# The last of four mLSTM heads: its instructions on VectorE, ScalarE and GpSimd put into a written order

## The chip, the core and the metric

The kernel runs on one NeuronCore of one Trainium2 chip, in one launch. The time is that of the device, in microseconds, from three runs; the profile is one further execution. The engines run their own in-order queues and meet only through semaphores: TensorE (PE, with its weight loads shown apart as PEld), VectorE (DVE), ScalarE (ACT), GpSimd (POOL), and SP, which here issues nearly all transfers.

## The reference

One layer of a hybrid backbone, batch 1, 1024 latent tokens (`x`) and 256 context tokens (`ctx`), width 1024. Only the latent stream is returned. Cut to what matters here:

```python
# adaLN-modulated RMSNorm, then one projection into all parts
hm, _, _ = mlstm_bidirectional(qm, km, vm, gates_x, st_f, st_b, True)     # 4 heads of width 128
y_m = mlstm_merge(hm, om, mlstm_norm[l])
y_a = window_attention(apply_rope(qa, cos, sin) * attn_scale, apply_rope(ka, cos, sin), va,
                       ka_c, va_c, attn_sink[l])                          # 8 query heads of width 64
x = x + g_a * (jnp.concatenate([y_m, y_a], axis=-1) @ w_out[l])
x = x + g_f * conv_glu(modulate(rmsnorm(x, norm_ffn[l]), sh_f, sc_f), ...)

def mlstm_merge(h, o, gain):
    hn = h * lax.rsqrt(jnp.mean(h * h, axis=-1, keepdims=True) + EPS)
    hn = hn.transpose(0, 2, 1, 3).reshape(b, l, MLSTM_W) * gain
    return (hn * jax.nn.sigmoid(o)).astype(o.dtype)
```

The mLSTM runs over chunks, forward and backward. Each chunk of a head has a state (128x128 matrix and a vector) from the chunks before it, and an inner part in which every pair of positions has a decay, an exponential under a causal mask. The output of a position is the sum of both directions, each divided by its own normaliser. `mlstm_merge` then divides by the root of the mean square over the 128 elements of the head, and multiplies by a gain and by the sigmoid of an output gate.

## The kernel before

**Stages.** First norm, modulation and shared projections; then the four mLSTM heads, one after the other; while head h runs its recurrence, TensorE does the dense projections of head h+1 (`dense`), and during the last head, which has no successor, the query projections of the attention (`qgen`). Then window attention with the output projection, then the convolutional GLU. A tile has 128 partitions; a chunk here is 128 tokens, so there are 8 latent chunks (`NL`) and 2 context chunks (`NC`).

**One head** is the generator `mlstm`. It `yield`s 30 times. Between two yields the loop at the bottom of the listing lets `dense` or `qgen` add some TensorE work: it keeps a debt, raised by `RATE` (1.5) or, in the last head, `RATE3` (0.37) per yield, and takes pieces of 0.64 from the other generator until the debt is paid. A query projection is four such pieces. In the order of the yields, counted n = 0 to 29:

- n = 0, 1: two chunks of k are transposed ahead (`tr`, L653), and ScalarE copies them out with two scales (L657, L659).
- n = 2 to 10: nine backward state steps, i = 0 to 8. Each transposes two chunks ahead, multiplies (L680), and VectorE adds to the state (L688, L690). Here stand also the loads of the decays' exponents (`ee_load`), the additions of the causal mask (`mask`, L663), the exponentials (`decay`, L667, ScalarE), the pieces in which the head before is finished (`next(fins[0])`), and the output gate: tanh on ScalarE over all 8 chunks (L703) and a product on VectorE (L704).
- n = 11, 12: two forward state steps over the context. n = 13: the first q-k product.
- n = 14 to 29: eight turns of two yields, one per latent chunk, numbered 0 to 7 here. `first` makes the q-k product of the next chunk and the next forward state (L722, L710, L715), and multiplies decays in (L725). `second` makes the output (L733 to L736 on TensorE), ScalarE scales the state's part (L739), VectorE adds (L740) and makes the normalisers (L742 to L744). Its `rest` comes one turn later: ScalarE and VectorE form `hid` (L747, L748), and, a yield later, ScalarE squares and sums it (L751) into `hss`.

```python
        for c in range(NC, NCH):
            if c + 1 < NCH:
                first(c + 1)
            if tail:
                next(tail)
            yield
            ...
            if tail:
                next(tail)
            tail = second(c)
            yield
```

`finish` ends a head: root of the mean square on ScalarE (L784, another activation table than the exponential's and the tanh's), reciprocal (L785), and eight scalings of 128x128 (L787) on VectorE. For heads 0 to 2 it is spread over the state steps of the next head; for the last head it follows at once.

**PSUM.** The transposes, state steps, q-k products and outputs of a head share one pool of four buffers (`pl`). After the last head that pool is closed and its four banks go to the attention's pools (`pT`, `pO`, `pU`), which the rest of `qgen` already uses for the transposes of q and k (L883, L857). In the same place the head's scratch memory is closed, and `wm` opens in it: the attention's keys (`kT2`), values (`vv`) and the output weights (`wor`). The first write there is ScalarE's L1032.

**Order.** The framework has a planner that orders each engine's instructions by estimated times. Inside `tc.manual_schedule(engines=...)` the engines named issue in the order in which the code writes them; how that region mixes with instructions written outside it stays with the planner. The loop over heads names TensorE always, and for heads 0 to 2 also VectorE, ScalarE, GpSimd and SP. So in the last head only TensorE has a written order.

**Query projections.** Weights for queries come in two sets. The second, `w_q[1]`, is loaded in the last head by `load_split`: two halves of 512 KB (L152), each cut into a high part (copy on ScalarE, L156) and a low part (subtraction on VectorE, L157). Each projected chunk is rotated by three VectorE instructions (L319, L319, L320), which free one of two PSUM buffers; then `qtrans` splits (L877 on ScalarE, L878 on VectorE), transposes, copies out (L885) and stores q (L886).

Of the kernel before, what the change touches and what calls it, by code (L numbers as in the profile page):

```python
# [9 lines left out]
F32 = mybir.dt.float32  # L10
# [8 lines left out]
P = 128  # L19
# [59 lines left out]
def build(tc, I, out, dbg=None):  # L79
# [553 lines left out]
    fins = []  # L633

    def mlstm(h, kT, qT, va):
# [32 lines left out]

        ahead = [tr(order[1][0])]
# [4 lines left out]
        for i, c in enumerate(order[1][:-1]):  # L674
# [22 lines left out]
            if i > 1:  # L697
                mask(i - 2)
            if i in (4, 6, 8):
                decay(i // 2 - 2)  # L700
            if i == TN:

                S.activation(yv, yv, AF.Tanh, scale=0.5)  # L703
                V.scalar_tensor_tensor(out=yv, in0=yv, scalar=1.0, in1=rwc("gain", h * DH, DH).unsqueeze(1)  # L704
                                       .broadcast_to([P, NL, DH]), op0=ALU.add, op1=ALU.mult)
# [22 lines left out]
        def second(c):  # L728
# [17 lines left out]
            def rest():  # L746
                S.activation(hid[:, b], nm[:, 0, 0:DH], AF.Copy, scale=dn[:, 0:1])  # L747
                V.scalar_tensor_tensor(out=hid[:, b], in0=nm[:, 1, 0:DH], scalar=dn[:, 1:2], in1=hid[:, b],  # L748
                                       op0=ALU.mult, op1=ALU.add)
                yield  # L750
                S.activation(nm[:, 0, 0:DH], hid[:, b], AF.Square, accum_out=hss[:, b:b + 1])  # L751
                yield
            return rest()

        for c in range(NC):
            pn = pl.tile([P, 512], F32, name="pn", tag="l")
            step(c, pn[:, 0:E1])
            if c == 0:
                cfs.clear()
            if c == 0:  # L760
                mask(NL - 1)
            decay(3 + c)
            yield
        first(NC)
        tail = None
# [27 lines left out]
        if h < H - 1:  # L793
            fins.append(finish())
        else:
            for _ in finish():
                pass

# [175 lines left out]
    for h in range(H):  # L977
# [3 lines left out]
        else:  # L981
            wq = [wkq]
            late = lambda: wq.append(load_split(I["w_q"][1], 256, lambda: pq.tile([P, 4, 256], F32, name="wr", tag="rga")))
# [14 lines left out]
        with tc.manual_schedule(engines=order_):  # L998
            dn = dense(h + 1, wkq, wvo, *nh) if nh else qgen()
            rate = RATE if nh else RATE3  # L1000
            for n, _ in enumerate(mlstm(h, *cur)):
                if nh is None and n == LW3:
                    late()
                    rga = pq.tile([P, D], F32, name="rga", tag="rga")
                    nc.sync.dma_start(rga[:], row(0))
# [17 lines left out]
            if nh is None:  # L1023
                mstk.close()
# [1158 lines left out]
```

## Time and profile before

| | us |
|---|---|
| three runs: lowest, median, highest | 1265.94, 1266.54, 1266.77 |
| profiled execution, its own time | 1265.89 |
| its span, first to last instruction | 1264.1 |
| mean granted TensorE clock | 0.998 |
| first mLSTM instructions of the last head, about | 322 |
| last scaling of the last head (L787) ends | 362.3 |

How to read the lines that follow: a timeline row has the start in us, the length in us, the engine, the line, the operation, output <- inputs, and the number of instructions merged; in brackets the idle time before it and what ended it. The length of one instruction runs from its start to its end, and the next may start before that end. A wait row names the engine, tile and line that waited, the one it waited for, the sum in us, how often, and the longest. PEld shows TensorE's weight loads, one for each product.

### The profile page before, as it was taken

Reading aid. Unit: us, or ns where it says so; the run is one execution under the profiler, and the core shown is the slowest. Engines: PE = TensorE matmul, PEld = TensorE weight load, DVE = VectorE, ACT = ScalarE, POOL = GpSimd, SP = SyncE. Lnnn points to the kernel's source line nnn. Section 1 sums busy time; section 2 is a strip of 40 time slices with the busy share of each in tenths; the row PEclk is TensorE's granted clock in tenths of the full one; section 3 lists DMA queues with packets and bytes.
Section 4 is the critical chain, followed back from the end, with each engine's and each line's share of the span. In section 5 each row is a group of like instructions: output and inputs, shape, how many; then the busy total and the mean of one; then the engine's idle time right before and its main releaser. Section 6 shows DMA issues by size and latency. Waiting matters only on the chain.

```text
span 1264.1 us, 19253 instructions
## 1 busy us (share of the span) xinstructions
PE 1234.4 (98%) x7047; PEld 1060.2 (84%) x7047; DVE 972.8 (77%) x1691; ACT 637.9 (50%) x1309; POOL 187.1 (15%) x162
## 2 busy tenths in 40 slices
PE   6999999999999999999999999999999999999997
PEld 4799999999898888888887888888888888788886
DVE  5873777777787888788987877777777777877887
ACT  6632556464865777776843333333333334434435
POOL 1200000000001443221002232133231232001000
PEclk9999999999999999999999999999999999999999
DMA  9541535362354333104313322223322237975553
GB/s 361 184 142 34 145 115 153 115 181 75 85 175 160 134 120 115 51 34 167 117 51 130 115 99 102 95 102 117 103 105 100 93 135 269 335 250 187 195 192 134
DMA packets 90560, 176.17 MB, mean 139 GB/s; under 512 B 12954, under 2 KB 29538, under 8 KB 90466
## 3 DMA queue, kind: packets, MB, share of 16 engines
q1 hardware_dynamic: 90178, 174.15, 41.2%
q8 instruction: 56, 0.92, 0.3%
q10 hardware_dynamic: 288, 0.79, 0.2%
q14 instruction: 38, 0.31, 0.1%
HBM read 136.58 MB, written 38.33 MB: 138 GB/s over the span
## 4 chain that ended last, share of the span: by engine, by line
PE 84%; DVE 6%; ACT 5%; DMA 3%; issue 2%; POOL 1%; SPq 0%; ACTq 0%; DVEq 0%; POOLq 0%
PE pd L2020 14%; PE pa L1480 8%; PE pc L1480 8%; PE pp L588 7%; PE pe L1480 4%; PE pd L1480 4%; PE pb L1480 4%; PE u L1182 3%; PE pv L307 2%; PE pv L309 2%; PE pv L308 2%; PE po L307 2%; PE po L309 2%; PE po L308 2%; PE pt L1159 2%
## 5 line engine op out<-in xcount | busy, mean ns | idle before, releaser
L1597 ACT CAST wh<-Rb 128x1024 fp32r<-128x1024 f32 (+1 forms) x63 | 56.8, 903 | 144.1 <-PE pd L1480 77.1
L2020 PE MATMUL pd<-dh,al 128*128 128x512 f32 x296 | 115.4, 390 | 0.9 <-DVE al L1361 0.9
L2020 PE MATMUL pd<-dl,ah 128*128 128x512 f32 x296 | 115.3, 389 | 0.0
L2020 PE MATMUL pd<-dh,ah 128*128 128x512 f32 x296 | 115.1, 389 | 0.0
L1480 PE MATMUL pc<-hB,wh 128*128 128x512 f32 x344 | 105.6, 389 | 0.0
L1480 PE MATMUL pa<-hB,wh 128*128 128x512 f32 x336 | 103.8, 390 | 0.2 <-ACT sn L1679 0.2
L1198 DVE TENSOR_TENSOR wl<-Rb,wh 128x1024 fp32r<-128x1024 f32 (+1 forms) x63 | 65.8, 1045 | 39.2 <-ACT wh L1597 38.6
L1715 POOL TENSOR_TENSOR tt<-vt,tt 128x512 f32<-128x512 f32 x22 | 29.5, 1341 | 367.5 <-ACT tt L1709 367.5
L588 PE MATMUL pp<-hl,wh 128*128 128x512 f32 x256 | 79.3, 405 | 0.0
L307 PE MATMUL pv<-wh,hl 128*128 128x256 f32 x256 | 75.9, 296 | 0.0
L1480 PEld LDWEIGHTS pc<-hB,wh 128*128 128x128 f32 x344 | 64.6, 188 | 13.5
L1480 PEld LDWEIGHTS pa<-hB,wh 128*128 128x128 f32 x336 | 62.9, 188 | 14.1 <-ACT sn L1679 1.1
L309 PE MATMUL pv<-wh,hl 128*128 128x256 f32 x256 | 72.4, 283 | 0.0
L308 PE MATMUL pv<-wl,hl 128*128 128x256 f32 x256 | 72.3, 282 | 0.0
L2020 PEld LDWEIGHTS pd<-dh,al 128*128 128x128 f32 x296 | 55.6, 188 | 13.1 <-DVE al L1361 1.6
L1480 PE MATMUL pc<-hB,wl 128*128 128x512 f32 x172 | 66.4, 389 | 0.0
L2020 PEld LDWEIGHTS pd<-dl,ah 128*128 128x128 f32 x296 | 55.5, 188 | 11.8 <-DVE dl L1361 0.3
L1480 PE MATMUL pa<-hB,wl 128*128 128x512 f32 x168 | 65.4, 389 | 0.0
L2020 PEld LDWEIGHTS pd<-dh,ah 128*128 128x128 f32 x296 | 55.6, 188 | 11.6
L1166 ACT CAST ph<-pt 128x512 fp32r<-128x512 f32 (+1 forms) x88 | 46.2, 525 | 25.3 <-PE pt L1159 25.0
L1136 DVE TENSOR_REDUCE nm<-sps 128x1 f32<-128x641 f32 (+1 forms) x64 | 50.3, 786 | 4.9 <-PE sps L1132 3.4
L1480 PE MATMUL pd<-hB,wh 128*128 128x512 f32 x176 | 54.0, 390 | 0.0
(1082 smaller groups left out, 3694.4 us busy)
## 6 DMA issues: line engine op xcount, KB each, us to landing
w<-in_w_ada_dram SPq DMA_DIRECT2D x64, 256.0 KB, 2.8
br<-in_w_down_dram SPq DMA_DIRECT2D x25, 512.0 KB, 5.9
ar<-act_s SPq DMA_DIRECT2D x44, 256.0 KB, 4.0
Ra<-in_w_up_dram SPq DMA_DIRECT2D x21, 512.0 KB, 3.6
Rb<-in_w_up_dram SPq DMA_DIRECT2D x21, 512.0 KB, 3.6
act_a<-tt SPq DMA_DIRECT2D x33, 256.0 KB, 2.0
act_s<-tt SPq DMA_DIRECT2D x33, 256.0 KB, 2.0
wr<-in_w_h_dram SPq DMA_DIRECT2D x16, 512.0 KB, 4.1
```

What stands on the lines that cost most here:

```text
L307: T.matmul(ps, st_hi, mv_hi, start=first, stop=False)
L308: T.matmul(ps, st_hi, mv_lo, start=False, stop=False)
L309: T.matmul(ps, st_lo, mv_hi, start=False, stop=last)
L588: T.matmul(pp[:, 512 * n:512 * n + 512], wkq[sw][:, kt, cs], hl[n][part][:, kt, :], start=kt == 0 and sw + part == 0, stop=kt == KT - 1 an ...
L1136: V.tensor_reduce(out=self.nm[:, j:j + 1], in_=self.sv[j], axis=AX.X, op=ALU.max, negate=True)
L1166: S.copy(self.ph[i][:, :w], self.pt[i][:, :w])
L1182: T.matmul(self.u[:], vv[:, c, self.g], part[i][:, kk * 2 * P:(kk + 1) * 2 * P], start=kb + m == 0, stop=kb == last and m == 1)
L1198: sub = lambda e, o, x, y: e.tensor_tensor(out=o, in0=x, in1=y, op=ALU.subtract)
L1480: T.matmul(ps[:, cols], wt[sw][:, j, kt * P:kt * P + P], hB[part][:, blk, kt, cols], start=first and n == 0, stop=last and n == len(seq) - ...
L1597: S.copy(wt[0][:], src)
L1715: G.tensor_tensor(out=self.tt[:, h2_], in0=self.vt[:], in1=self.tt[:, h2_], op=ALU.mult)
L2020: T.matmul(ps[:], ac[sa][:, js], w[sw], start=first and n == 0, stop=last and n == 2, skip_group_check=not fresh)
```

## The change

- The last head gets a written order on VectorE, ScalarE and GpSimd too (`inner`), ended when its generator is exhausted. SP stays with the planner there.
- In the last head the masks and exponentials come two state steps later (`late_ = 2`), and the output gate (`gate`, the old L703 and L704) moves from the eighth state step to the square of chunk 2, that is, to n = 21.
- Head 2 isn't finished piece by piece in the last head. `gated` multiplies its hidden values by its gate in one 128x1024 VectorE instruction, written at i = 1, and keeps its sums of squares. The last head does the same at its end, and then both heads are finished together: two roots, two reciprocals, two products of 128x1024.
- `w_q[1]` is no longer loaded and cut in one place (n = 12). Its first half is issued at n = 6 and cut at n = 13, where the second is issued; that is cut at n = 20, and the row of the residual's gate (`rga`) is loaded there.

```diff
--- before.py
+++ after.py
@@ -630,7 +630,7 @@
         if h == 0:
             dump("kT", kT[:]); dump("qT", qT[:]); dump("va", va[:].rearrange("p c e -> p (c e)"))
 
-    fins = []
+    fins, held = [], []
 
     def mlstm(h, kT, qT, va):
         cbk = tp.tile([P, NL, DH + 1], F32, name="cbk", tag="cbk", bufs=1)
@@ -666,6 +666,12 @@
             for d in range(2):
                 S.activation(ee[:, b, d], ee[:, b, d], AF.Exp, bias=g1(a_, d, NC + b), scale=-1.0)
 
+        def gate():
+            S.activation(yv, yv, AF.Tanh, scale=0.5)
+            V.scalar_tensor_tensor(out=yv, in0=yv, scalar=1.0, in1=rwc("gain", h * DH, DH).unsqueeze(1)
+                                   .broadcast_to([P, NL, DH]), op0=ALU.add, op1=ALU.mult)
+
+        late_ = 2 if h == H - 1 else 0
         ahead = [tr(order[1][0])]
         yield
         ahead.append(tr(order[1][1]))
@@ -694,15 +700,12 @@
                 ee_load(2 * i + 2)
             if fins and i:
                 next(fins[0])
-            if i > 1:
-                mask(i - 2)
-            if i in (4, 6, 8):
-                decay(i // 2 - 2)
-            if i == TN:
-
-                S.activation(yv, yv, AF.Tanh, scale=0.5)
-                V.scalar_tensor_tensor(out=yv, in0=yv, scalar=1.0, in1=rwc("gain", h * DH, DH).unsqueeze(1)
-                                       .broadcast_to([P, NL, DH]), op0=ALU.add, op1=ALU.mult)
+            if i > 1 + late_:
+                mask(i - 2 - late_)
+            if i in (4 + late_, 6 + late_, 8):
+                decay((i - late_) // 2 - 2)
+            if i == TN and not late_:
+                gate()
             yield
         cf, cfs = [None], []
 
@@ -749,6 +752,8 @@
                                        op0=ALU.mult, op1=ALU.add)
                 yield
                 S.activation(nm[:, 0, 0:DH], hid[:, b], AF.Square, accum_out=hss[:, b:b + 1])
+                if late_ and b == 2:
+                    gate()
                 yield
             return rest()
 
@@ -757,11 +762,18 @@
             step(c, pn[:, 0:E1])
             if c == 0:
                 cfs.clear()
-            if c == 0:
-                mask(NL - 1)
-            decay(3 + c)
+            if late_:
+                mask(5 + c)
+                decay(2 + c)
+            else:
+                if c == 0:
+                    mask(NL - 1)
+                decay(3 + c)
             yield
         first(NC)
+        if late_:
+            mask(NL - 1)
+            decay(4)
         tail = None
         yield
         for c in range(NC, NCH):
@@ -790,15 +802,25 @@
                     yield
             fins.clear()
             yield
-        if h < H - 1:
+
+        def gated():
+            V.tensor_tensor(out=yv, in0=hid[:], in1=yv, op=ALU.mult)
+            held.append((hss, yv))
+            fins.clear()
+            yield
+        if h < H - 2:
             fins.append(finish())
+        elif h < H - 1:
+            fins.append(gated())
         else:
-            for _ in finish():
+            for _ in gated():
                 pass
-
-
-
-
+            for s_, _ in held:
+                S.activation(s_[:], s_[:], AF.Sqrt, bias=eps_t[:], scale=1.0 / DH)
+            for s_, _ in held:
+                V.reciprocal(s_[:], s_[:])
+            for s_, y_ in held:
+                V.tensor_tensor(out=y_, in0=y_, in1=s_[:].unsqueeze(2).broadcast_to([P, NL, DH]), op=ALU.mult)
 
     def ada_second():
         R4 = 4 * KT
@@ -980,7 +1002,8 @@
             order_ |= {mybir.EngineType.DVE, mybir.EngineType.Activation, mybir.EngineType.Pool, mybir.EngineType.SP}
         else:
             wq = [wkq]
-            late = lambda: wq.append(load_split(I["w_q"][1], 256, lambda: pq.tile([P, 4, 256], F32, name="wr", tag="rga")))
+            wq1 = lambda: load_split(I["w_q"][1], 256, lambda: pq.tile([P, 4, 256], F32, name="wr", tag="rga"), split=False,
+                                     alloc=False, now=(0,))
             for _ in ada:
                 pass
             V.scalar_tensor_tensor(out=ada2[:, 16:24], in0=ada2[:, 16:24], scalar=1.0, in1=spc("nffn", 0, KT), op0=ALU.add, op1=ALU.mult)
@@ -998,9 +1021,17 @@
         with tc.manual_schedule(engines=order_):
             dn = dense(h + 1, wkq, wvo, *nh) if nh else qgen()
             rate = RATE if nh else RATE3
+            if nh is None:
+                inner = tc.manual_schedule(engines={mybir.EngineType.DVE, mybir.EngineType.Activation, mybir.EngineType.Pool})
+                inner.__enter__()
             for n, _ in enumerate(mlstm(h, *cur)):
-                if nh is None and n == LW3:
-                    late()
+                if nh is None and n == LW3 - 6:
+                    late = wq1()
+                if nh is None and n == LW3 + 1:
+                    late((0,))
+                    late.load(1)
+                if nh is None and n == LW3 + 8:
+                    wq.append(late((1,)))
                     rga = pq.tile([P, D], F32, name="rga", tag="rga")
                     nc.sync.dma_start(rga[:], row(0))
                 if nh and n in (2, LW):
@@ -1021,6 +1052,7 @@
                         break
                     debt -= w
             if nh is None:
+                inner.__exit__(None, None, None)
                 mstk.close()
                 plk.close()
                 pl = pT = pa_.enter_context(tc.tile_pool(name="pT", bufs=2, space=PSUM))
```

## The prediction

> **What bounds the kernel now.** I read the head of the page first, then stretches of 10 us around the last head, then who is waited for there, then single rows.
>
> ```profile
> span 1264.1 us, 19253 instructions
> ...
> PE 1234.4 (98%) x7047; PEld 1060.2 (84%) x7047; DVE 972.8 (77%) x1691; ACT 637.9 (50%) x1309; POOL 187.1 (15%) x162
> ```
>
> TensorE (PE) is busy 98% of the span. Its instruction list is written out by hand before and after, and the change adds and removes no product. So the time moves by what TensorE waits, and by nothing else. The last head starts near 322 us. The stretches give, in columns, the length, then PE, PEld, DVE, ACT and POOL busy, the clock, the DMA share and GB/s:
>
> ```profile
> 322.00:332.00 10.00, 8.43 (x63) 7.21 (x62) 7.77 (x26) 8.96 (x25) 0.00 (x0) 1.00 0.72 160
> 332.00:342.00 10.00, 9.61 (x82) 9.42 (x83) 9.65 (x34) 9.13 (x29) 0.00 (x0) 1.00 0.15 54
> 342.00:352.00 10.00, 9.21 (x81) 9.05 (x81) 9.42 (x37) 7.08 (x25) 0.00 (x0) 1.00 0.14 55
> ```
>
> PEld, the weight loads, shows a gap best. It lacks 2.8 us in the first stretch and 1.5 in the two others together. VectorE (DVE) is nearly full from 332 on: there the planner has packed other work between its dependent instructions. GpSimd has no instruction here, so its written order costs nothing. Who held the weight loads between 322 and 334 us, the backward state steps:
>
> ```profile
> PEld pn L653 <- DVE cbk L690: 1.4, 4, 0.5
> PEld pn L680 <- ACT kwf L659: 1.0, 2, 0.6
> PEld pn L653 <- DVE cst L688: 0.9, 1, 0.9
> ```
>
> That is 3.3 us in seven gaps, all of them waits for an instruction that stood too late in VectorE's or ScalarE's queue. This is what the change can win.
>
> **The start of the last head.** The rows that price it, VectorE's first, then ScalarE's:
>
> ```profile
> 335.51 0.42 DVE L319 TENSOR_TENSOR ta<-px,rope 128x256 f32<-128x256 f32 x1
> 335.84 0.41 DVE L319 TENSOR_TENSOR z<-px,rope 128x256 f32<-128x256 f32 x1
> 336.18 0.42 DVE L725 SCALAR_TENSOR_TENSOR ee<-pe,ee 128x256 f32<-128x256 f32 x1
> 336.64 1.22 DVE L157 TENSOR_TENSOR wl<-wr,wh 128x1024 fp32r<-128x1024 f32 x1
> 337.79 0.42 DVE L320 TENSOR_TENSOR z<-z,ta 128x256 f32<-128x256 f32 x1
> 338.12 0.42 DVE L878 SCALAR_TENSOR_TENSOR qs<-z,qs 128x256 fp32r<-128x256 f32 x1
> ...
> 339.05 0.41 DVE L740 TENSOR_TENSOR nm<-pi,nm 128x258 f32<-128x258 f32 x1
> ...
> 355.04 0.42 DVE L740 TENSOR_TENSOR nm<-pi,nm 128x258 f32<-128x258 f32 x1
> ...
> 360.11 2.18 DVE L787 SCALAR_TENSOR_TENSOR ym<-hid,hss,ym 128x128 f32<-128x128 f32 x8
> ```
>
> ```profile
> 323.46 1.04 ACT L703 ACTIVATE ym<-ym 128x1024 f32<-128x1024 f32 x1
> ...
> 326.10 1.28 ACT L784 ACT_TABLE_LOAD   x1
> ...
> 330.08 1.28 ACT L667 ACT_TABLE_LOAD   x1
> ```
>
> Starts that follow on each other give what one instruction takes from the queue: 0.33 for each of a rotation's three and for the remainder behind it (L319, L319, L320, L878), 1.15 for a 128x1024 pass (L157).
>
> Gone from here: ScalarE's tanh (1.04) and VectorE's gate product, both moved behind turn 2; with the third head's root two table loads (2.57); its eight scalings. Added: one 128x1024 product of the third head (1.15), as long as the gate's. The masks keep their number. They come two steps later, so that the first state step no longer stands behind masks that wait for their transfer (the 0.9 above).
>
> The eight scalings are priced by the last head's own (L787, 2.18). The first turn's VectorE sum (L740) stands at 339.05 now. VectorE is nearly full up to it, so without the scalings and the wait for the masks it comes at about 339.05 - 2.1 - 0.9 = **336.1**. TensorE's gaps allow the same: 339.05 - 3.3 = 335.8. I bound it by 335.4 and 336.8, the first half of the query weights' split (1.15, now always ahead of the first turn) and ScalarE's bunched masks' exponentials being what could be late. The transfers stay with the planner on the SP queue. The second half of the weights is issued after the first split and needed seven half turns later; the turns cover it, and uncovered it would cost the time to its landing. Behind it on SP stand the row of the residual's gate and q stores, which come only from turn 6 on.
>
> **The eight turns in written order.** This is the term that decides. Heads 0 to 2 already run in written order, with the same turn, and TensorE gives them so much other work that it does not show. One turn of the third head, VectorE, then ScalarE:
>
> ```profile
> 289.35 0.42 DVE L740 TENSOR_TENSOR nm<-pi,nm 128x258 f32<-128x258 f32 x1
> ...
> 290.89 0.35 DVE L748 SCALAR_TENSOR_TENSOR hid<-nm,dn,hid 128x128 f32<-128x128 f32 x1
> ...
> 298.24 0.43 DVE L740 TENSOR_TENSOR nm<-pi,nm 128x258 f32<-128x258 f32 x1 [0.88 <-ACT nm L739]
> ```
>
> ```profile
> 290.46 0.40 ACT L747 ACTIVATE hid<-nm,dn 128x128 f32<-128x128 f32 x1 [1.83 <-DVE dn L744]
> ...
> 291.35 0.30 ACT L751 ACTIVATE nm<-hid 128x128 f32<-128x128 f32 x1
> 291.55 0.19 ACT L751 ACTIVATION_READ_ACCUMULATOR nm<-hid 128x1 f32 x1
> ...
> 297.58 0.63 ACT L739 ACTIVATE nm<-pj,gi 128x129 f32<-128x129 f32 x2 [0.45 <-PE pj L734]
> ```
>
> In the code a turn writes, in this order: L747 and L748 of the turn before, L751 of the turn before, then L739 and L740 of its own. In an in-order queue that is a ring. L740 to L747 takes 290.46 - 289.35 = 1.11; L747 to L751, through L748 on VectorE, 0.89; L751 with its read 291.74 - 291.35 = 0.39; L739 to L740 298.24 - 297.58 = 0.66. Together 3.05, and nothing of it can overlap the next turn. One mask's exponential lies in that turn; without it I take **3.0**.
>
> From the L740 at 339.05 to that at 355.04 seven turns take 15.99 now, 2.28 each with two rotations and a weight split among them: the planner has broken the ring, as it could with L739 of a turn ahead of the L751 written before it. In written order seven take 21.0, plus what now stands in the ring:
> - After turn 2's sum a rotation with its remainder, 4 x 0.33, all of it between L744 and L715 of turn 2, and L748 waits behind them: +1.3.
> - Behind L748 of turn 2 the second weight split (ScalarE's copy runs early, VectorE's 1.15 stays), then the gate: L751 is done 0.85 after L748's start (291.74 - 290.89), then tanh 1.04, the product 1.15. L740 of turn 3 follows at 3.0 instead of 0.85 + 0.66 = 1.5: +1.5.
> - After L748 of turn 5 (0.35) the next rotation, 1.3, against the 1.5 that ScalarE takes meanwhile; and ScalarE has two more instructions ahead of L751: +0.4, an estimate from L747's 0.40.
>
> Together 24.2. The turns count from 0, so L740 of the last turn comes at 336.1 + 24.2 = 360.3 instead of 355.04: **+5.3**.
>
> **Who waits for it.** After the last turn the four PSUM buffers of the head's pool are handed to the attention's pools, and the first transposes there stand in TensorE's list behind the fifth query projection.
>
> ```profile
> 355.51 0.72 PEld L883 LDWEIGHTS pt<-identr,qs 128*128 128x128 f32 x8
> ```
>
> L740 ended at 355.04 + 0.42 = 355.46 and the transposes began at 355.51: TensorE has no slack against that last read. Its own list doesn't help: the products of the last turn wait for L725 behind the sixth turn's L740. So TensorE goes on 5.3 later, and at 98% busy it has nothing to catch up with.
>
> **The end of the head.** The scratch memory that the next stage writes is also freed by the last scaling, as ScalarE's wait shows:
>
> ```profile
> 362.37 1.28 ACT L1032 ACT_TABLE_LOAD   x1 [2.13 <-DVE ym L787]
> ```
>
> That is 7.33 after L740 of the last turn. New: 1.54 to L748 and 0.85 to the end of L751, one table load 1.28, two roots (0.6, by the 0.30 of L751, a bound from a wider instruction), two reciprocals (0.3, below that), two passes of 1.15 and 1.22; the output product lies under the load. That is 6.9, so the release comes at about 367.3, +5.0: behind TensorE's +5.3 and costing nothing more. Without that cover it could cost up to the same 5.0, not on top.
>
> **The sum.** 1265.89 of the profiled execution, whose span is 1264.1, plus 5.3 is 1271.2. The median of the runs, 1266.54, lies 0.65 above that execution, so I forecast **1271.9**.
>
> **The rivals.**
>
> *Late rotation (slower still).* The fifth projection's rotation is written behind the region; the planner may place it behind the two final passes. TensorE's seventh projection, which starts when these transposes end, at 359.6,
>
> ```profile
> 359.16 0.46 PE L883 MATMUL pt<-identr,qs 128*128 128x128 f32 x4
> ```
>
> would then wait for 367.3 and for the rotation's two reads, 0.8 more: +8.5, 1275.0. For it: two passes stand at that place, 2.4 against 2.18. Against: there are idle spots while the table loads. 13%.
>
> *The ring hides (no change).* Turns keep their 2.28 and only the moved work counts: 336.1 + 16.0 + 3.2 = 355.3, +0.3, so 1266.9. For it: the mean turn of today; against: the order in the code leaves no way for it. 10%.
>
> *Faster.* The price of the turn is met by VectorE's sheer work, which today fills it, and not by the ring; the moved work lies in the holes too. Then the head's last L740 comes 339.05 - 336.1 = 2.95 earlier, the release follows, and the time is 1263.6. It decides where the turns stay under about 2.2. For it: TensorE and VectorE are the fuller engines. Against: 3.05 is built of waits between engines, not of busy time. [...] 12%.
>
> **How the numbers follow.** The forecast has 65%. Its own range takes turns from 2.8 to 3.1, the start's bounds and 2.0 to 4.5 for what stands in the ring: +2.0 to +8, 1268.5 to 1274.6. For 8 in 10 I reach down over the no-change case and up over the late rotation: 1265.5 to 1275.5, leaving out most of the faster case and a little above. A difference under 0.2%, 2.5 us, can't be told from none in this kernel. Faster 0.13, the same 0.11, slower 0.76.
>
> **What would show it.** In the changed profile: no gaps at L653 and L680 early in the head, L740 of the first turn near 336; then L740 every 3.0 us, ended by "ACT nm L739", and VectorE under 80% busy; TensorE idle some 9 us between 334 and 361 (the 3.3 won ahead of it, the 5.3 lost, and little that is there today); no root's table load before 360. If L740 comes every 2.3 us, the ring is wrong and with it the sign.

## The result, and the profile after

The changed kernel takes **1276.43 us** (median of 6 runs, 1274.84 to 1278.36) against 1266.49 (1265.93 to 1267.08) for the kernel before on the same chip: ratio 1.0079, 95% interval 1.0069 to 1.009. It is slower by 9.9 us. The forecast had the sign and the mechanism of the turns, but with +5.3, and the measured time lies above the end of its range, 1275.5. The profiled execution takes 1276.98, 11.1 more than the one of before.

Line numbers move with the change: the turn's sum L740 is now L743, its scaling L739 is L742, the reciprocal L744 is L747, the row's halves L747 and L748 are L750 and L751, the square L751 is L754; the attention's first transposes L883 are L905.

The head of the page of the changed kernel:

```profile
span 1275.2 us, 19233 instructions
...
PE 1239.1 (97%) x7047; PEld 1064.7 (83%) x7047; DVE 976.2 (77%) x1679; ACT 634.6 (50%) x1307; POOL 186.5 (15%) x162
```

VectorE and ScalarE have fewer instructions and the span is 11.1 longer. The stretches, as before in columns the length, PE, PEld, DVE, ACT, POOL, the clock, the DMA share and GB/s:

```profile
322.00:332.00 10.00, 9.84 (x83) 9.38 (x81) 7.97 (x26) 7.96 (x30) 0.00 (x0) 1.00 0.76 161
332.00:342.00 10.00, 9.66 (x78) 9.01 (x77) 8.27 (x26) 6.58 (x24) 0.00 (x0) 1.00 0.15 52
342.00:352.00 10.00, 6.78 (x42) 6.36 (x42) 7.85 (x23) 5.37 (x16) 0.00 (x0) 0.83 0.17 55
352.00:362.00 10.00, 6.69 (x56) 6.26 (x54) 7.28 (x27) 5.00 (x18) 0.00 (x0) 0.97 0.07 27
362.00:372.00 10.00, 9.78 (x62) 9.60 (x62) 5.75 (x13) 5.07 (x11) 0.00 (x0) 0.69 0.29 93
```

Before, the last two of these stretches were full and at full clock:

```profile
352.00:362.00 10.00, 10.00 (x90) 9.94 (x89) 7.20 (x29) 7.07 (x20) 0.00 (x0) 1.00 0.32 111
362.00:372.00 10.00, 10.00 (x90) 9.88 (x89) 8.37 (x18) 7.40 (x15) 0.00 (x0) 1.00 0.73 224
```

The first stretch is won as forecast. The third and fourth are lost to waits, the third also to a clock of 0.83. The fifth is new: TensorE is busy for 9.78 us and yet does 62 products instead of 90, because the granted clock is 0.69.

The turns' sums on VectorE:

```profile
336.72 0.42 DVE L743 TENSOR_TENSOR nm<-pi,nm 128x258 f32<-128x258 f32 x1
339.64 0.43 DVE L743 TENSOR_TENSOR nm<-pi,nm 128x258 f32<-128x258 f32 x1 [1.03 <-ACT nm L742]
342.58 0.43 DVE L743 TENSOR_TENSOR nm<-pi,nm 128x258 f32<-128x258 f32 x1 [1.03 <-ACT nm L742]
348.45 0.42 DVE L743 TENSOR_TENSOR nm<-pi,nm 128x258 f32<-128x258 f32 x1
351.33 0.43 DVE L743 TENSOR_TENSOR nm<-pi,nm 128x258 f32<-128x258 f32 x1 [0.98 <-ACT nm L742]
354.21 0.43 DVE L743 TENSOR_TENSOR nm<-pi,nm 128x258 f32<-128x258 f32 x1 [0.98 <-ACT nm L742]
357.49 0.42 DVE L743 TENSOR_TENSOR nm<-pi,nm 128x258 f32<-128x258 f32 x1
361.48 0.43 DVE L743 TENSOR_TENSOR nm<-pi,nm 128x258 f32<-128x258 f32 x1 [0.98 <-ACT nm L742]
```

A plain turn takes 2.88 to 2.94, and what ends VectorE's wait is ScalarE's scaling, as the ring says. Then the first transposes, and the next ones, on the weight loads:

```profile
362.03 1.07 PEld L905 LDWEIGHTS pt<-identr,qs 128*128 128x128 f32 x8 [3.54 <-issue]
...
368.17 0.41 PEld L905 LDWEIGHTS pt<-identr,qs 128*128 128x128 f32 x4
```

The "issue" is no releaser; the waits of the products themselves name the sum:

```profile
PE pt L905 <- DVE nm L743: 3.4, 1, 3.4
```

Before, these groups began at 355.51 and 359.06. They are 6.5 and then 9.1 late. What lies between, 2.6, is the clock, in stretches of 2 us:

```profile
360.00:362.00 2.00, 0.00 (x0) 0.00 (x0) 0.85 (x4) 1.03 (x5) 0.00 (x0) 0.83 0.00 0
362.00:364.00 2.00, 1.94 (x12) 1.97 (x13) 0.70 (x4) 1.19 (x3) 0.00 (x0) 0.50 0.00 0
...
366.00:368.00 2.00, 2.00 (x11) 2.00 (x11) 0.20 (x1) 0.63 (x3) 0.00 (x0) 0.50 0.05 15
368.00:370.00 2.00, 2.00 (x20) 2.00 (x20) 1.53 (x3) 0.59 (x1) 0.00 (x0) 0.96 0.00 0
```

Since TensorE runs the same products in the same order, its lag can be read everywhere. The table gives, for some products, when they start before, and how many us later (minus: earlier) the same product starts in each kernel. I worked it out by matching TensorE's rows one by one, in one profiled execution of each kernel; the last row is the difference of the spans. The kernels of the other columns come below.

```
start before   after  planner  order   square   dummies  dummies  filled
                               only    later      (40)     (30)
   322.0       -0.1    -0.2     0.2     0.7      0.1     -0.1      0.6
   334.6       -3.0    -3.3    -0.3    -2.1     -2.7     -3.0     -2.3
   344.4       -1.1    -2.8    10.5    -0.8     -0.8     -1.0     -0.3
   354.2        3.1    -3.3    12.9     1.4      3.6      3.4      3.8
   356.2        6.9    -2.8    16.7     2.8      7.9      6.9      3.1
   364.2        9.5    -2.8    18.7     2.8      7.9      7.1      5.2
   376.8        8.9    -3.5    18.8     3.3      7.2      6.7      5.9
   398.3       10.7    -1.7    18.4     3.0      8.5      8.8      7.3
   550.3       10.8      -       -       -       8.5      8.9      7.4
   span        11.1    -1.4    19.1     3.3     10.9     14.0      7.3
```

The row at 322 lies ahead of everything that was changed. The lag there, -0.2 to +0.9 over all traces of this case, was nearly all made in the first 30 us of the execution, so differences of under 1 us between two columns are to be read against it.

So of the 11.1 of the changed kernel 10.7 are made by 400 us: 6.5 up to the end of the wait for the last sum, 2.6 while the clock is down (the table's 356.2 lies 0.7 us into that), 0.4 at the third transposes, and, after 0.6 have been made up, 1.8 between 377 and 398.

### The profile page after: what moved, and what is told of

Its sections match the earlier page's. It is cut to its first block, busy times and chain, and to the rows that moved or that the text cites. A ratio compares the mean times of both kernels' runs of the same rounds, so it can differ in the third digit from the quotient of the medians.

```text
span 1275.2 us, 19233 instructions
## 1 busy us (share of the span) xinstructions
PE 1239.1 (97%) x7047; PEld 1064.7 (83%) x7047; DVE 976.2 (77%) x1679; ACT 634.6 (50%) x1307; POOL 186.5 (15%) x162
## 4 chain that ended last, share of the span: by engine, by line
PE 83%; DVE 6%; ACT 4%; DMA 4%; issue 2%; SPq 1%; POOL 1%; ACTq 0%; DVEq 0%; POOLq 0%
PE pd L2052 14%; PE pa L1512 8%; PE pc L1512 8%; PE pp L588 7%; PE pe L1512 4%; PE pd L1512 4%; PE pb L1512 4%; PE u L1214 3%; PE pv L307 2%; PE pv L309 2%; PE pv L308 2%; PE po L307 2%; PE po L309 2%; PE po L308 2%; PE pt L1191 2%
## 5 line engine op out<-in xcount | busy, mean ns | idle before, releaser
L1230 DVE TENSOR_TENSOR wl<-Rb,wh 128x1024 fp32r<-128x1024 f32 (+1 forms) x63 | 65.9, 1048 | 39.2 <-ACT wh L1629 38.6
L307 PE MATMUL px<-wh,hl 128*128 128x256 f32 (+1 forms) x176 | 54.1, 307 | 0.2 <-ACT xT L238 0.2
```

Source lines behind the costliest of these rows:

```text
L307: T.matmul(ps, st_hi, mv_hi, start=first, stop=False)
L1230: sub = lambda e, o, x, y: e.tensor_tensor(out=o, in0=x, in1=y, op=ALU.subtract)
```

## The experiments

**The order alone and the moves alone.** The first kernel leaves out the written order, and the planner orders the three engines again:

```
-                inner = tc.manual_schedule(engines={DVE, Activation, Pool})
-                inner.__enter__()
+                inner = ExitStack()
```

> The changed kernel with the written order of the last head taken away again: VectorE, ScalarE and GpSimd go back to the planner, while the later masks and exponentials, the later gate, the roots taken together and the split load of the query weights stay. Ring theory (the order of the rows L754 and L742 on ScalarE costs the time): the turns go back to about 2.3 us and the time to 1264 to 1268. Moved-work theory (the later gate, the two long products and the split load cost it): most of the 9.9 us stays, 1272 to 1276.

The second is the kernel before with the written order and none of the moves:

```
+            if nh is None:
+                inner = tc.manual_schedule(engines={DVE, Activation, Pool})
+                inner.__enter__()
```

> The kernel before with nothing but the written order on VectorE, ScalarE and GpSimd in the last head; masks, gate, finish of the third head and load of the query weights as before. Ring theory: turns of about 2.9 us again and a last sum L740 near 360, so 1270 to 1276, with TensorE at half clock behind its longest wait. Moved-work theory: within 2.5 us of before, 1264 to 1269. If it is clearly slower than the changed kernel, the moves of the change are a help to the written order.

Measured: 1264.29, ratio to before 0.9984 (0.9975 to 0.9993), and 1284.08, 1.0139 (1.0125 to 1.0153). The order alone lies above the ranges of both theories. The moves by themselves are a small gain, and the written order costs 12.1 with them (1276.43 - 1264.29) and 17.9 without (1284.08 against 1266.22 for the kernel before in the same comparison). The kernel before measured 1265.99 to 1266.85 in the five comparisons, so a difference between kernels of two of them is uncertain by up to that 0.9. With the planner the ring is broken: the last sum comes at 352.22, and TensorE barely waits.

```profile
352.68 0.72 PEld L905 LDWEIGHTS pt<-identr,qs 128*128 128x128 f32 x8 [0.48 <-DVE nm L743]
```

With the order alone, the old place where both halves of the query weights are loaded and split stands ahead of the first turn. ScalarE's row and TensorE's:

```profile
342.09 1.04 ACT L156 CAST wh<-wr 128x1024 fp32r<-128x1024 f32 x1 [5.00 <-DMA wr<-in_w_q_dram]
```

```profile
346.25 0.93 PEld L736 LDWEIGHTS pi<-va,ee 128*128 128x128 f32 x4 [8.34 <-DVE ee L725]
```

In written order ScalarE waits 5.00 for the second half of the weights, the split on VectorE waits behind it, and what the first turn's products need stands behind that. TensorE's lag grows from -0.3 to 10.5 there. So the moved load is what the written order misses most, as far as these rows show; no run put that load alone back.

**The ring.** In the last head the square of a turn is written behind the next turn's sum:

```
-            if tail:
+            if tail and not late_:
                 next(tail)
-            tail = second(c)
+            new = second(c)
+            if tail and late_:
+                next(tail)
+            tail = new
```

> The changed kernel with one exchange in the last head: the square of a chunk (L754) is written behind the next turn's scaling and sum (L742, L743) instead of ahead of them. All work and all other order stays. Ring theory: the ring loses L751 to L754 and the read, and a turn costs L743 to L750 1.1, L750 0.3 and L742 to L743 0.7, that is 2.1, or VectorE's own 2.2; the last L743 comes some 5 us earlier, TensorE's wait goes, and with it the half clock: 1264 to 1269. Rival, VectorE's list in itself is the bound: turns stay near 2.9 and the time at 1274 to 1277.

Measured: 1268.99, ratio 1.0017 (1.0008 to 1.0026); one of the eleven runs took 3163 us and is left out of the ratio. One instruction of eight turns, moved, gives back 7.4 of the 9.9. The sums follow at 2.6 in the first plain turns, where 2.1 to 2.2 was expected, the last one comes at 357.72, 3.8 earlier, and the wait is too short to bring the clock down (1.00 in each stretch of 4 us from 344 to 372).

```profile
358.27 0.73 PEld L908 LDWEIGHTS pt<-identr,qs 128*128 128x128 f32 x8 [1.45 <-issue]
```

Then I moved the two halves of the row as well:

```
-            if tail:
+            if tail and not late_:
                 next(tail)                # in both places
...
+            new = second(c)
+            if tail and late_:
+                next(tail)
+                next(tail)
```

> The changed kernel with the written order kept, but in the last head's turns both halves of the turn before (the two instructions that make the normalized row, and its square) are written behind the turn's own sum. Ring theory: what is left of the loop is sum to reciprocal 0.86, second product 0.35, square with its read 0.39, ScalarE's scaling to the sum 0.66, together 2.3 a turn instead of 2.9. Last sum near 355.5, no wait of TensorE for it above 1 us, no stretch at half clock, and a time of 1266 to 1269, at or under the 1269.0 of the kernel that moved the square alone. Rival, VectorE's sheer work bounds the turns: nothing beyond that kernel, 1269 to 1270. Rival, the order is dear for another reason than the loop: 1272 or more.

Measured: 1274.4, 1.0064 (1.005 to 1.0077); the last sum comes at 359.57. My expectation of 1266 to 1269 fell. A plain turn is 2.4 as worked out (350.03 to 352.43), but ScalarE's square now waits for a VectorE instruction that stands behind the sum of the turn, and where the gate, the weight split and the rotations lie in between, all of them enter the loop. ScalarE's row ahead of the gate, and TensorE's behind it:

```profile
346.91 0.31 ACT L754 ACTIVATE nm<-hid 128x128 f32<-128x128 f32 x1 [1.91 <-DVE hid L751]
```

```profile
349.90 0.30 PEld L736 LDWEIGHTS pj<-cst,qT 128*128 128x128 f32 x2 [2.32 <-ACT hid L750]
```

**Two parts within the written order.** The gate back ahead of the turns, and each head its own root and scalings:

```
-            if i == TN and not late_:
+            if i == TN:
                 gate()
...
-                if late_ and b == 2:
-                    gate()
```

> The changed kernel with the output gate's tanh and product back where they were, at the fifth forward state step ahead of the turns; all else kept. Ring theory: the turn that now holds the gate falls from 5.9 to about 3.0, the first sum comes up to 2.2 later, since ScalarE and VectorE have the gate ahead of it, so that the last sum comes 0.7 to 2.9 earlier than 361.5, TensorE waits 0.6 to 2.8 instead of 3.5 there, no half clock behind it, and the time is 1270 to 1274. Rival, the gate costs the same wherever it is written: 1276 to 1277.

```
-        if h < H - 2:
+        if h < H - 1:
             fins.append(finish())
-        elif h < H - 1:
-            fins.append(gated())
         else:
-            for _ in gated():
+            for _ in finish():
                 pass
```

> The changed kernel with each of the last two heads taking its own root, reciprocal and eight scalings as in the kernel before; all else kept. Ring theory: the third head's eight scalings (2.2 on VectorE, less the 1.15 product they replace) and its two activation table loads (2.6 on ScalarE) stand ahead of the first turn, so the first sum comes 1.0 to 2.6 later than 336.7 and the last as much later than 361.5; the end of the head costs about the same. Time 1277.5 to 1279.5. Rival, taking the roots together is worth nothing: 1276 to 1277. Rival, it costs, since the two wide products at the end hold the release: 1275 or less.

Measured: 1277.53, 1.0089 (1.0076 to 1.0103), and 1277.34, 1.0086 (1.0072 to 1.0099). Neither can be told from the changed kernel's 1.0079. The first and the last sum, with the gate early, then with own roots:

```profile
339.18 0.42 DVE L743 TENSOR_TENSOR nm<-pi,nm 128x258 f32<-128x258 f32 x1
...
362.44 0.43 DVE L743 TENSOR_TENSOR nm<-pi,nm 128x258 f32<-128x258 f32 x1 [0.98 <-ACT nm L742]
```

```profile
339.96 0.42 DVE L743 TENSOR_TENSOR nm<-pi,nm 128x258 f32<-128x258 f32 x1
...
364.74 0.43 DVE L743 TENSOR_TENSOR nm<-pi,nm 128x258 f32<-128x258 f32 x1 [0.98 <-ACT nm L742]
```

The early gate makes the first sum 2.5 later and its turn 1.5 shorter: the last sum is 1.0 later, 0.6 of it a lag that was there at 322. I had expected it earlier and 1270 to 1274, so the rival holds that the gate costs the same wherever it is written. Own roots make both sums 3.2 to 3.3 later, 0.7 of it there at 322; the 2.6 left is the upper end of what I expected. The time is just under the 1277.5 that I had as the lower end. TensorE's lag at 398 is only 11.3 against 10.7: it lost 1.4 behind the wait, where the changed kernel lost 2.6, and nothing between 377 and 398. The clock was down for 3.4 us there and for 6.8 in the changed kernel; the last section shows why.

**More work for TensorE in the turns.**

```
-RATE3 = 0.37
+RATE3 = 0.47
```

> The changed kernel with the rate at which query projections are drawn into the last head's turns raised from 0.37 to 0.47 per step, so that TensorE has about one projection more, some 3 us of work, ahead of the wait for the last sum. Clock theory: that wait falls from 3.5 to 1 us or less, no stretch at half clock, what follows is already done, and the time comes 2.5 to 5 us down, to 1271 to 1274, though the last sum itself comes up to 0.8 later by the extra rotation in the loop. Rival, only the last sum's place counts: the time stays at 1276 to 1278. Rival, the extra rotations stretch the loop by more than the projection is worth: above 1278.

Measured: 1276.69, 1.0084 (1.007 to 1.0097). My expectation of 1271 to 1274 fell. The wait stayed at 3.55: the last sum came at 364.58, 3.1 later. Of that 0.9 was there at 322; for the rest, with each projection its rotation goes into the loop too, and the first turn takes 4.28 instead of 2.92. The lag at 398 is 10.5. Work that brings VectorE work into the ring fills nothing.

**The clock and the wait.** TensorE gets 40 dummy transposes at the place where it waits, and in a second kernel 30:

```
+            if t == 4:
+                sp_ = pk.tile([P, SEQ], F32, name="spun", tag="pp")
+                for _ in range(40):       # 30 in the second kernel
+                    T.transpose(sp_[:, 0:P], ident[:], ident[:])
```

> The changed kernel with 40 transposes of a constant, read by nobody, added on TensorE where it waits 3.5 us for the last L743 ahead of L905. They fill that wait and end with it. Clock theory (the idle time makes the granted clock fall to a half for the 6 us behind it, which costs 2.6 us): the clock stays at 1.0 there, the last L743 stays at about 361.5, and the time falls by 2 to 3 us to about 1273.5. Rival, the half clock comes from something else or costs nothing because what follows waits anyway: no change, 1275 to 1278.

> The changed kernel with 30 dummy transposes in TensorE's wait instead of the 40, which had run 0.9 us past the last sum. If the half clock costs what the trace shows and the earlier kernel with dummies lost it by another accident of the planner: no stretch at half clock, TensorE 2.6 us earlier behind the wait, 1273.5 to 1274.5. If the half clock is made up for later: 1276 to 1277.

Measured: 1276.82, 1.0082 (1.0069 to 1.0096), and 1277.98, 1.009 (1.0077 to 1.0104). By the times alone the clock would cost nothing, and both expectations of the clock theory fell. The traces show what it costs TensorE at that place. With 40 dummies the clock stays up behind the wait:

```profile
360.00:362.00 2.00, 2.00 (x20) 2.00 (x19) 0.91 (x4) 1.32 (x5) 0.00 (x0) 1.00 0.06 12
362.00:364.00 2.00, 2.00 (x23) 2.00 (x21) 1.30 (x6) 0.44 (x2) 0.00 (x0) 1.00 0.00 0
```

and the table's lag does not grow behind the wait (7.9 and 7.9; 6.9 and 7.1), where the changed kernel's grows from 6.9 to 9.5. Up to 550 both kernels are 1.9 to 2.3 less late than the changed one. They lose it again far behind: 0.6 and 1.7 between 600 and 630, and 1.5 and 3.3 at 1070 to 1081, the start of the down projection. There VectorE waits longer for a transfer of weights (L1230, with the dummies L1234), and TensorE for VectorE. The changed kernel, then 40 dummies (with 30 the wait is 2.04):

```profile
1083.45 1.23 DVE L1230 TENSOR_TENSOR b<-b,br 128x1024 f32<-128x1024 f32 x1 [0.41 <-DMA br<-in_w_down_dram]
```

```profile
1083.30 1.23 DVE L1234 TENSOR_TENSOR b<-b,br 128x1024 f32<-128x1024 f32 x1 [1.94 <-DMA br<-in_w_down_dram]
```

With 30 dummies the clock falls there too, and that makes 1.6 of the 3.3:

```profile
1086.50:1089.90 3.40, 1.47 (x4) 0.66 (x4) 3.40 (x4) 1.57 (x2) 0.00 (x0) 1.00 1.05 387
1089.90:1093.31 3.41, 3.41 (x9) 2.68 (x9) 3.38 (x4) 2.29 (x3) 0.00 (x0) 0.50 1.03 381
```

It is not another plan: by the timelines every engine has the same instructions in the same order from 405 us on, in these kernels and the changed one. Why the transfer came late is not settled. The profiled execution with 30 dummies, 1279.86, is also the slowest of its four. So these two runs show what the clock costs where it falls, and leave open what of it reaches the end. The next kernel puts useful products in the wait: the transposes are held back by one projection.

```
-    def push(g):
+    def push(g, lag=None):
         next(g)
         qpend.append(g)
-        if len(qpend) > LAG:
+        while len(qpend) > (LAG if lag is None else lag):
             next(qpend.pop(0), 0)
...
-                push(qtrans(*qseq[t - 1]))
+                push(qtrans(*qseq[t - 1]), 9 if t == 4 else None)
...
-                push(kgens.pop(0))
+                push(kgens.pop(0), 9 if t == 4 else None)
```

> The changed kernel, in which TensorE takes the sixth query projection (24 products, 2.9 us at full clock) ahead of the transposes that wait for the last sum, so that its wait of 3.5 us is filled with work that has to be done anyway; nothing else is moved on VectorE, ScalarE or in the transfers by hand. If TensorE's lost time sets the end: the wait falls to about 0.6, no half clock, TensorE stands 2.9 + 2.6 = 5.5 us earlier behind it, and the time is 1271 to 1273. If the wait's own length sets it and the half clock is made up for later: 1273 to 1274. If the late release and the transfers behind it set it: 1275.5 to 1277.

Measured: 1273.66, 1.0061 (1.0049 to 1.0074). The last sum came 0.75 later than in the changed kernel (362.23), 0.7 of it there at 322, and yet the time is 2.8 lower and the span 3.8. TensorE waits 0.67 and stays at full clock (1.00 from 356 on):

```profile
362.77 0.73 PEld L905 LDWEIGHTS pt<-identr,qs 128*128 128x128 f32 x8 [0.67 <-PE px L309]
```

The lag behind the wait is 5.2 instead of 9.5, at 398 it is 7.3, and the span shows the same 7.3. So TensorE's lost time does reach the end, and not the last sum's place as such. The time is not in the range that I gave for that (1271 to 1273) but in the one for a half clock that is made up for later (1273 to 1274): of the 4.3 won at 364, part goes again between 364 and 398. By the time alone the filled wait of some 2.9 explains the gain, so this run does not show the clock's part of it separately.

The same edit on the kernel with the later square, and on the one with the planner's order:

> The kernel with the written order and the square moved behind the next turn's sum (1269.0), with the same projection ahead of the waiting transposes. Its wait there was 1.45 and no half clock followed. If TensorE's lost time sets the end: 1267.3 to 1268.0. If not: 1268.8 to 1269.5.

> The kernel with all moves but without the written order (1264.3), with the sixth projection ahead of the transposes. TensorE waited only 0.5 us there, so 1263.8 to 1264.8 if the planner's order stays the same; the transposes themselves come 2.9 us later, and if what hangs on them matters, up to 1267.

Measured: 1271.74, 1.0037 (1.0023 to 1.0051), and 1264.22, 0.9981 (0.9972 to 0.999). Where the wait was only 1.45 the filling costs 2.75 in time (1271.74 - 1268.99); expected was a gain or nothing. The held-back transposes now come in a bunch, TensorE waits for ScalarE's copies out of their buffers, and the clock is at 0.50 from 363.6 to 367.0:

```profile
363.36 0.46 PEld L908 LDWEIGHTS pt<-identr,qs 128*128 128x128 f32 x4 [2.75 <-ACT QTo L910]
```

With the planner the edit changes nothing.

**What the moves are worth with the planner.** Four kernels, each with the planner's order and one move taken back: own roots and early gate as in the diffs above, the masks and their exponentials two steps earlier, and the query weights loaded and split in one place:

```
-            if i > 1 + late_:
-                mask(i - 2 - late_)
+            if i > 1:
+                mask(i - 2)
...
```

```
-                if nh is None and n == LW3 - 6:
-                    late = wq1()
-                if nh is None and n == LW3 + 1:
-                    late((0,))
-                    late.load(1)
-                if nh is None and n == LW3 + 8:
-                    wq.append(late((1,)))
+                if nh is None and n == LW3:
+                    late()
```

> The kernel with all moves but without the written order (1264.3), and in it each of the last two heads taking its own root, reciprocal and eight scalings as before. If the roots taken together carry the gain over the kernel before: VectorE has the eight scalings of the third head (2.2) ahead of the first turn again and ScalarE two table loads more, the backward state steps wait again in part, and the time goes back by 1 to 2 us, to 1265.3 to 1266.5. If the masks or the query weights carry it: 1264.0 to 1264.8.

> The kernel with all moves but without the written order (1264.3), and in it the output gate back at the fifth forward state step. If the late gate carries the gain: tanh 1.04 and product 1.15 stand ahead of the first turn again, 1265.3 to 1266.5. If the planner finds room for the gate anyway: 1264.0 to 1264.8.

> The kernel with all moves but without the written order (1264.3), and in it the masks and their exponentials at the steps of the kernel before, two earlier. If the later masks carry the gain: TensorE waits again some 1 to 2 us for the backward state steps, 1265.3 to 1266.5. If they don't: 1264.0 to 1264.8.

> The kernel with all moves but without the written order (1264.3), and in it the second half of the query weights loaded and split at one place as in the kernel before. I expect nothing of it, 1264.0 to 1264.8, since the planner places transfers and splits itself. If the split load carries the gain: 1265.3 or more.

Measured, against 1266.62: 1266.47 (ratio 0.9992 to 1.0009), 1266.07 (0.9987 to 1.0004), 1266.01 (0.9989 to 1.0006) and 1268.07 (1.0001 to 1.0019). Each one taken back loses most of the gain of 2 or more than it, so the four are not a sum; for the gate and the masks the intervals still touch that of all moves (0.9975 to 0.9993). TensorE's lag at 335 is -3.3 with all moves and +0.5, -1.0, -2.3 and -2.4 with one taken back; from 322 on it falls by 3.0 with all moves and by 0.0, 1.5, 2.4 and 2.3: the roots count most there. For the weights I had expected nothing; the old place is dearest. Its lag goes from -2.4 at 336 to +1.3 by 340, where the clock is at 0.50 from 337.4 on. A further 2.1 come between 595 and 630, where the order is the same; that execution, 1270.2, is itself 2.1 above the median of its kernel.

The fastest kernels are the two with all moves and without the written order: 1264.29 and 1264.22, 2 to 3 us under the kernel before.

## Why the prediction was right, and where not

- **The start.** Forecast 336.1 for the first sum, at most 336.8; it came at 336.72. The waits at L653 and L680 (now L686) between 322 and 334 fell from 3.3 to

```profile
PEld pn L653 <- DVE cbk L696: 0.6, 2, 0.3
```

- **The ring.** Forecast 3.0 a turn; measured 2.88 to 2.94. The turn with rotation, weight split and gate: forecast 3.0 + 1.3 + 1.5 = 5.8, measured 5.87. The turn with the next rotation: 3.4 and 3.28. The square moved out of the loop took most of the loss away, and the planner's order all of it; the ring is shown.
- **The last turn.** I had 3.0 and it took 3.99. A rotation (L319, L319, L320) and a remainder (L900) came to stand in it, the rotation with a wait:

```profile
358.72 0.42 DVE L319 TENSOR_TENSOR ta<-px,rope 128x256 f32<-128x256 f32 x1 [0.41 <-PE px L309]
```

With the start's 0.6 the last sum was 6.4 later instead of 5.3.
- **"So TensorE goes on 5.3 later, and at 98% busy it has nothing to catch up with."** This is the step that failed, and with it the premise that the time moves by what TensorE waits "and by nothing else". The lateness was right in kind (6.5 at the transposes), but the step took a wait of 3.5 us to cost 3.5 and put the clock behind it at nothing. The clock was at 0.50 for 6.1 us of the work behind it, and the next transposes were 2.6 later still. With the clock kept up by dummies the lag does not grow there. That is TensorE's lag at this place: no run shows the 2.6 by itself in the time, since both kernels with dummies came out no faster.
- **"Behind TensorE's +5.3 and costing nothing more."** This failed too. The release was forecast at 367.3. VectorE's rows:

```profile
366.16 0.20 DVE L821 RECIPROCAL hss<-hss 128x8 f32<-128x8 f32 x1 [0.82 <-ACT hss L819]
368.47 0.42 DVE L319 TENSOR_TENSOR ta<-px,rope 128x256 f32<-128x256 f32 x1 [2.10 <-PE px L309]
368.81 0.19 DVE L821 RECIPROCAL hss<-hss 128x8 f32<-128x8 f32 x1
368.92 2.31 DVE L823 TENSOR_TENSOR ym<-ym,hss 128x1024 f32<-128x1024 f32 x2
```

A rotation that waits 2.10 for TensorE's projection, itself at half clock, stands between the two reciprocals. The products end at 371.23, 8.9 later than before. It is my rival of the late rotation, in mirror image: not the rotation behind the products but the products behind the rotation. The transfers behind the release are late in turn. The fourth load of the output weights on the SP queue, the product that waits for it, and the transposes behind that product, in the changed kernel:

```profile
391.42 0.34 SPq L913 DMA_DIRECT2D wor<-in_w_out_dram  x1
```

```profile
396.75 1.23 DVE L918 TENSOR_TENSOR wor<-wor,rga 128x1024 f32<-128x1024 f32 x1 [1.56 <-DMA wor<-in_w_out_dram]
```

```profile
401.44 0.40 PEld L905 LDWEIGHTS pt<-identr,qs 128*128 128x128 f32 x4 [1.45 <-issue]
```

Before, the same load was issued at 379.93 and the product did not wait:

```profile
379.93 0.46 SPq L891 DMA_DIRECT2D wor<-in_w_out_dram  x1
```

```profile
385.42 1.21 DVE L896 TENSOR_TENSOR wor<-wor,rga 128x1024 f32<-128x1024 f32 x1
```

It is issued 11.5 later, more than the release is late; how much of that is the release and how much the planner's place on SP wasn't tried apart. TensorE's wait behind it is 1.45. The 0.4 at the third transposes is a wait for the remainder L900, which stands at 371.48 behind the two final products.
- **The rivals.** "Ring hides" and "faster" fell with the sums. "Late rotation" had about the time (1275.0), for another reason.

The sum as measured: 6.5 at the end of the wait, +2.6 for the clock, +0.4 at the third transposes, -0.6 made up, +1.8 from 377 to 398 (1.5 of it at that load), +0.4 later: 11.1.

## What to carry to other kernels

Before an in-order list is written by hand, follow one value around through all engines: what the list makes serial is paid in every turn, here 0.6 a turn, and one instruction written later gave most of it back. A wait of TensorE near 3.5 us is to be priced with the slow clock behind it, and so are two shorter ones close together. It is best filled with products that have to be done anyway, if the wait is as long as they are. A difference of 1 to 3 us may arise hundreds of us behind the edit, where every engine's order is the same as before; a running lag shows where it arises, the total does not, and one profiled execution is not the median.

## What the runs showed of the hardware

The granted clock changes on a fixed grid. In the changed kernel it falls at 347.68, returns at 351.09, falls at 361.33 and returns at 368.16; any two of these lie a whole number of 3.41 us apart. The same holds within each of the 18 traces of this case, for all 70 changes in them. Where the grid lies differs from execution to execution.

So the clock's fall is not a matter of the length of one gap alone. In the changed kernel two gaps of 1.48 and 1.57 between 344 and 348 lie between the same two points of the grid, and 0.50 follows:

```profile
344.27:347.68 3.41, 0.88 (x6) 0.52 (x5) 3.12 (x7) 2.51 (x6) 0.00 (x0) 1.00 0.00 0
347.68:351.09 3.41, 3.25 (x15) 3.25 (x16) 2.57 (x8) 1.22 (x6) 0.00 (x0) 0.50 0.47 156
```

With 30 dummies, which come only later, the same two gaps (1.48 and 1.57, at the same places within 0.04) fall into two stretches of the grid, and the clock stays up:

```profile
342.38:345.79 3.41, 1.87 (x14) 1.68 (x15) 3.04 (x11) 1.84 (x4) 0.00 (x0) 1.00 0.00 0
345.79:349.20 3.41, 2.00 (x15) 1.84 (x16) 3.06 (x6) 1.86 (x5) 0.00 (x0) 1.00 0.29 111
```

I took TensorE's busy share of every such stretch in all 18 traces (the ends of products are modelled in a trace, so the shares are rough). At full clock, each of the 30 stretches with a share of 0.45 or less was followed by the half clock (18 of them at the very end of the program). Of those with 0.51 or more only two were, both at 26.3 us with 0.84. Between 0.45 and 0.51 it went either way. At half clock, a stretch with 0.88 or more was followed by full clock, one with 0.79 or less by another slow one. The changed kernel's wait reaches 0.7 us into the first slow stretch (share 0.79), so there were two of them; with own roots the wait ends just ahead of the point, and there was one.

After the wait of 3.5 the clock was down each time that nothing filled it. The Trainium skill, TensorE: Matmul & The Clock Gate, section "HAM oscillation — how this bites in real kernels", gives the rule that TensorE should have no idle gap above about 3.4 us. The trace agrees for the gap of 3.5; the two shorter gaps that lowered it once and once not are not covered by that rule.
